# Scores of a windowed attention: two fp32r matmuls over split queries and keys, replaced by one float32 matmul on four array tiles

## The chip, the cores and the metric

One core of a Trainium2 chip. The metric is the time of one execution on the device in microseconds (us). TensorE (PE) multiplies, VectorE (DVE) and ScalarE (ACT) work elementwise, GpSimd (POOL) makes masks, and the SP queue starts most transfers.

## The reference

A decoder layer for 2048 positions and 1024 channels: half of the mixing channels go through a gated linear recurrence (4 heads), the other half through a sliding-window attention (8 query heads, 2 key/value heads of 64 channels); then an output projection, a gated feed-forward part with a short convolution, and a last normalisation. All in float32. The change touches the scores alone:

```python
scores = jnp.einsum('bnqhgd,bnkhd->bnhgqk', qb, kb) * scale   # blocks of 128 queries, 256 keys
dist = qi + ATT_BLOCK - kj
band = (dist >= 0) & (dist < WINDOW)                           # WINDOW = 128
scores = jnp.where(mask[None, :, None, None], scores, -jnp.inf)
m = jnp.maximum(jnp.max(scores, axis=-1, keepdims=True), sink)
p = jnp.exp(scores - m)
denom = jnp.sum(p, axis=-1, keepdims=True) + jnp.exp(sink - m)
```

Each block of 128 queries sees its own 128 keys and the 128 before. Of these 256 the band keeps exactly 128 for each query: keys at its own place or earlier in its own block, and later ones in the block before.

## The kernel before, in words

The sequence is worked in two halves of 1024 positions (`hf`). For each half there is a mixing stage (recurrence and attention, about 60 to 360 us and 1090 to 1410 us in the profile), an output projection (`out_proj`), and the feed-forward part (`gate_up`, `down`). The large products run as fp32r matmuls over operands that are split in a high and a low part (`unit`: hi·hi, hi·lo and lo·hi, 128 x 512 each, line 222; `project_v`, lines 750 to 752).

In the mixing stage a string of steps (`ORDER`) says in which order the generators are advanced: `H0` to `H3` are the recurrence's heads (`hgrn`), `A0` to `A3` the pairs of attention heads (`attend`), `V` the values' projection, `G` a gate's weights. A pair `j` holds one query head of each key/value head, the first in partitions 0 to 63, the second in 64 to 127 (`rows(kv)`). The order in which the instructions stand on each engine in the end is set by a scheduler that runs when the program is built, so a change in one place moves instructions around it.

The recurrence uses float32 matmuls on parts of the array: `pdiag` (128 rows, four tiles of 32 columns), `plev` (tiles of 32 or 64 columns). The attention's output product `poT` (line 541) uses two tiles of 64 columns. `pkn`, `pu`, `po`, `ppt`, `pot` are float32 with the whole array.

`attend` works on 512 queries at a time (`g`), for each kv head separately. It makes qh (fp32r) and ql (the rest) from q: qh stands in both halves of the partitions, and so does ql. `att_keys` makes the matching keys `KS`: for each kv, the high part in the head's own 64 rows and the low part in the other 64. A matmul of qh with `KS` then gives hi·hi and hi·lo at once, one of ql with `KS` the other two. For every two blocks of queries (`i0`) the scores go to one PSUM bank of the ring `at` (two banks, also used by `pv`, `ppt` and `poT`). From there ScalarE copies the scores of the earlier 128 keys to `sc`, and VectorE's predicated copy (mask `C.own`) puts those of the own block over them where the band says so: 128 numbers for each query are left. Then come the maximum, the exponentials and the sums, the transposes (`ppt`) and `poT`.

Of the kernel before, what the change touches and what calls it, by code (L numbers as in the profile page):

```python
# [17 lines left out]
P = 128  # L18
# [3 lines left out]
HALF = 1024  # L22
# [31 lines left out]
def hymba_layer(ctx: ExitStack, tc: tile.TileContext, a: dict, out: bass.AP):  # L54
# [19 lines left out]
    def ps(kind, name):  # L74
        return spaces[kind].tile([P, 512], F32, tag=kind, name=name)
# [33 lines left out]
    kc = cp.tile([P, 2, P], F32R, name="kcarry")  # L109
# [319 lines left out]
    def rows(kv):  # L429
        return slice(kv * HD, (kv + 1) * HD)  # L430

    def att_keys(hf, kv, invb, p):

        KS = p.tile([P, 2, P + HALF], F32R, name="KS")
        V = p.tile([P, 1 + TT, P], F32, name="V")
        if hf:
            nc.vector.tensor_copy(KS[:, :, 0:P], kc)  # L440
            nc.vector.tensor_copy(V[:, 0], vc)
        kT, vT = [p.tile([P, HALF], F32, tag="t4", name=n, bufs=2) for n in ("kT", "vT")]
        for jj, dst in ((ATT_J, kT), (ATT_J + 1, vT)):
            o = kv[jj - ATT_J]
            for b, bs in halves():
                nc.vector.tensor_tensor(dst[:, bs], o[b], invb[:, bs], op=ALU.mult)
                nc.scalar.activation(dst[:, bs], dst[:, bs], AF.Identity, bias=C.battn[:, jj:jj + 1])
        for kv in range(2):
            r, other = rows(kv), rows(1 - kv)
            nc.scalar.copy(KS[r, kv, P:], kT[r])  # L450
            nc.vector.tensor_tensor(KS[other, kv, P:], kT[r], KS[r, kv, P:].bitcast(F32), op=ALU.subtract)
        for b in range(NB):
            pv = ps("at", "pv")
            for i in range(4):
                t0 = (b * 4 + i) * P
                nc.tensor.transpose(pv[:, i * P:(i + 1) * P], vT[:, t0:t0 + P], ident)
            nc.scalar.copy(V[:, 1 + 4 * b:5 + 4 * b].rearrange("p a b -> p (a b)"), pv)
        if hf + 1 < NH:
            nc.vector.tensor_copy(kc, KS[:, :, HALF:HALF + P])
            nc.vector.tensor_copy(vc, V[:, TT])  # L460
        return KS, V

    def attend(hf, j, X, invb, KS, V, mix, p):

        o = unit(a["w_att"][j], X, "q")
        qT = slot(f"att{j}")
        for b, bs in halves():
            nc.vector.scalar_tensor_tensor(qT[:, bs], o[b], 0.125, invb[:, bs], op0=ALU.mult, op1=ALU.mult)
            nc.scalar.activation(qT[:, bs], qT[:, bs], AF.Identity, bias=C.bq[:, j:j + 1])
        yield  # L470
        scs = []
        for g in range(NB):
            sc = p.tile([P, 2, 4, P], F32, tag="sc", name="sc", bufs=2)
            gs = slice(g * 512, (g + 1) * 512)
            for kv in range(2):
# [3 lines left out]
                nc.scalar.copy(qh[r], qT[r, gs])  # L479
                nc.scalar.copy(qh[other], qT[r, gs])  # L480
                nc.vector.tensor_tensor(ql[r], qT[r, gs], qh[r].bitcast(F32), op=ALU.subtract)
                nc.scalar.copy(ql[other], ql[r].bitcast(F32))
                for i0 in (0, 2):
                    pb = ps("at", "psc")
                    first = hf == 0 and g == 0 and i0 == 0
                    for i in range(2):
                        n = g * 4 + i0 + i
                        w0 = 1 if first and i == 0 else 0
                        o = pb[:, i * 256 + w0 * P:(i + 1) * 256]
                        ks = slice((n + w0) * P, (n + 2) * P)  # L490
                        for t, qx in enumerate((qh, ql)):
                            nc.tensor.matmul(o, qx[:, (i0 + i) * P:(i0 + i + 1) * P], KS[:, kv, ks],
                                             start=t == 0, stop=t == 1)
                    pv = pb.rearrange("p (i w k) -> p i w k", i=2, w=2)
                    dst = sc[:, kv, i0:i0 + 2]
                    if first:
                        nc.vector.memset(dst[:, 0], NEG)
                        nc.scalar.copy(dst[:, 1], pv[:, 1, 0])
                    else:
                        nc.scalar.copy(dst, pv[:, :, 0])  # L500
                    nc.vector.copy_predicated(
                        dst, C.own.bitcast(U32).unsqueeze(1).to_broadcast([P, 2, P]), pv[:, :, 1])
# [13 lines left out]
            nc.scalar.activation(es, es, AF.Exp)  # L516
            nc.vector.tensor_tensor(den, den, es, op=ALU.add)
            nc.vector.reciprocal(den, den)
            nc.vector.tensor_tensor(sc, sc, den.unsqueeze(3).to_broadcast([P, 2, 4, P]), op=ALU.mult)
            scs.append(sc)  # L520
        yield
        for g, sc in enumerate(scs):
            pm = []
            for kv in range(2):
                pm.append([p.tile([P, 4, P], F32, tag="pp", name=n, bufs=4) for n in ("po", "pp")])
                pt = ps("at", "ppt")
                for i in range(4):
                    nc.tensor.transpose(pt[:, i * P:(i + 1) * P], sc[:, kv, i], ident)
                ptv = pt.rearrange("p (i q) -> p i q", i=4)
                for dst, mk in zip(pm[kv], (C.ownT, C.prevT)):  # L530
                    nc.vector.tensor_tensor(dst, ptv, mk.unsqueeze(1).to_broadcast([P, 4, P]), op=ALU.mult)
            oT = ps("at", "poT")
            first = None
            for i in (3, 2, 1, 0):
                n = g * 4 + i
                noprev = hf == 0 and n == 0
                for prev in (0,) if noprev else (1, 0):
                    for kv in (1, 0):
                        r = rows(kv)
                        with tc.issue_after(first) if first else ExitStack():  # L540
                            mm = nc.tensor.matmul(oT[r, i * P:(i + 1) * P], V[:, n + 1 - prev, r], pm[kv][prev][:, i],
                                                  start=noprev or prev == 1, stop=prev == 0)
# [706 lines left out]
    for hf in range(NH):  # L1249
        X, kv, invb, rs, f0 = nxt  # L1250
        with ExitStack() as st:
            p = pool(f"mix{hf}", stack=st, reuse_waits="tile")
            KS, V = att_keys(hf, kv, invb, p)
# [4 lines left out]
            pairs = [attend(hf, j, X, invb, KS, V, mix, p) for j in range(ATT_J)]  # L1258
# [85 lines left out]
```

## Time and profile before

| | us |
|---|---|
| median of 3 runs (lowest, highest) | 2125.06 (2124.44, 2128.92) |
| the profiled execution | 2124.22 |
| its span, first to last instruction | 2122.6 |
| TensorE busy in it | 2108.1 |
| VectorE, ScalarE busy | 1624.3, 1096.2 |

A matmul's busy time runs from its start to its modelled end, and matmuls overlap, so the sum over a group says less than the distance between starts; the timeline and the chain of waits give that. A plain float32 matmul of the program stands as two records in the trace (two passes over it), an fp32r one as one. In the timeline a row `x4` merges four neighbours, and its second number is the time from the first start to the last end.

### The profile page before, as it was taken

How to read it: one execution, taken by the hardware profiler on the slowest of the kernel's cores; microseconds unless marked ns; L12 is line 12 of the kernel's file. 1: busy time of each engine (PE TensorE's matmuls, PEld its weight loads, DVE VectorE, ACT ScalarE, POOL GpSimd, SP SyncE). 2: the span in 40 equal slices, each digit the busy share in tenths (PEclk: the TensorE clock that was granted, in tenths of full speed). 3: DMA queues.
4: the chain of work that ended last, by engine and by line, in shares of the span. 5: the costliest groups of instructions: out<-in, count | busy, mean ns of one | idle time of the engine just before them, and what ended most of it. 6: DMA issues, size and time to landing. Idle time of an engine off the chain costs nothing.

```text
span 2122.6 us, 29885 instructions
## 1 busy us (share of the span) xinstructions
PE 2108.1 (99%) x11584; PEld 1748.9 (82%) x11584; DVE 1624.3 (77%) x2374; ACT 1096.2 (52%) x1880; POOL 22.3 (1%) x52
## 2 busy tenths in 40 slices
PE   9999999999999999999999999999999999999998
PEld 7888888888888888888888888888888888878888
DVE  7457787898878878775863677868988787887766
ACT  6456575664434444335734476656544444443453
POOL 1000000000000000000000000000000000000000
PEclk9999999999999999999999999999999999999999
DMA  4111111523332325955731010213223223279643
GB/s 160 43 40 43 33 47 47 173 75 101 107 116 85 126 88 190 393 199 168 233 105 52 31 36 31 81 49 142 95 90 124 94 95 119 85 242 372 228 134 134
DMA packets 96475, 255.21 MB, mean 120 GB/s; under 512 B 17355, under 2 KB 19659, under 8 KB 96333
## 3 DMA queue, kind: packets, MB, share of 16 engines
q1 hardware_dynamic: 91076, 251.32, 34.4%
q10 hardware_dynamic: 5256, 1.98, 0.4%
q8 instruction: 91, 1.49, 0.3%
q14 instruction: 52, 0.42, 0.1%
HBM read 195.11 MB, written 57.16 MB: 119 GB/s over the span
## 4 chain that ended last, share of the span: by engine, by line
PE 97%; DVE 1%; ACT 1%; DMA 1%; issue 0%; SPq 0%; DVEq 0%; ACTq 0%
PE pop L222 8%; PE X L933 8%; PE X L934 8%; PE X L935 7%; PE q L222 4%; PE g L222 4%; PE f L222 4%; PE hq L222 4%; PE Y L935 4%; PE Y L933 4%; PE Y L934 4%; PE pdx L1151 3%; PE pdx L1153 3%; PE pdx L1152 3%; PE pdy L1151 3%; PE pdy L1152 3%
## 5 line engine op out<-in xcount | busy, mean ns | idle before, releaser
L758 ACT CAST whi<-raw 128x1024 fp32r<-128x1024 f32 x88 | 92.7, 1053 | 102.9 <-PE X L934 61.1
L933 PE MATMUL X<-T,whi 128*128 128x512 f32 x352 | 137.1, 389 | 0.0
L934 PE MATMUL X<-T,whi 128*128 128x512 f32 x352 | 136.9, 389 | 0.0
L935 PE MATMUL X<-T,wlo 128*128 128x512 f32 x352 | 136.9, 389 | 0.0
L1032 DVE SCALAR_TENSOR_TENSOR y<-ga,cw,y 128x1024 f32<-128x1024 f32 x88 | 112.6, 1281 | 28.4 <-ACT y L1030 28.2
L940 ACT COPY u<-X 128x512 f32<-128x512 f32 x88 | 51.7, 588 | 124.4 <-PE X L935 124.3
L200 ACT CAST whi<-raw 128x1024 fp32r<-128x1024 f32 x57 | 59.5, 1050 | 101.2 <-PE hq L222 33.5
L201 DVE TENSOR_TENSOR wlo<-raw,whi 128x1024 fp32r<-128x1024 f32 x57 | 69.4, 1222 | 54.8 <-ACT whi L200 54.5
L759 DVE TENSOR_TENSOR wlo<-raw,whi 128x1024 fp32r<-128x1024 f32 x88 | 107.4, 1221 | 0.3 <-ACT whi L758 0.3
L222 PE MATMUL pop<-XL,whi 128*128 128x512 f32 x256 | 88.7, 392 | 0.0
L631 ACT COPY G<-QK 128x1024 f32<-128x1024 f32 x48 | 51.4, 1070 | 71.7 <-DVE QK L653 66.5
L222 PE MATMUL pop<-XH,wlo 128*128 128x512 f32 x256 | 88.4, 391 | 0.0
L759 DVE TENSOR_TENSOR xld<-raw,xhd 128x1024 fp32r<-128x1024 f32 x72 | 81.1, 1134 | 9.3 <-ACT xhd L758 9.1
L222 PE MATMUL pop<-XH,whi 128*128 128x512 f32 x256 | 87.9, 394 | 0.0
L758 ACT CAST xhd<-raw 128x1024 fp32r<-128x1024 f32 x72 | 69.6, 978 | 27.1 <-DMA raw<-act0T 7.4
L933 PEld LDWEIGHTS X<-T,whi 128*128 128x128 f32 x352 | 66.1, 188 | 14.1 <-ACT u L940 0.4
L935 PEld LDWEIGHTS X<-T,wlo 128*128 128x128 f32 x352 | 66.1, 188 | 13.8
L934 PEld LDWEIGHTS X<-T,whi 128*128 128x128 f32 x352 | 66.0, 188 | 13.7
L1151 PE MATMUL pdx<-xhd,hid 128*128 128x512 f32 x192 | 74.5, 392 | 1.5 <-ACT xhd L758 0.9
L1152 PE MATMUL pdx<-xld,hid 128*128 128x512 f32 x192 | 74.7, 389 | 0.0
L653 DVE TENSOR_TENSOR QK<-QK,f 128x1024 f32<-128x1024 f32 x56 | 68.6, 1225 | 6.7 <-ACT G L631 5.9
L1153 PE MATMUL pdx<-xhd,lod 128*128 128x512 f32 x192 | 73.7, 389 | 0.0
(394 smaller groups left out, 6329.5 us busy)
## 6 DMA issues: line engine op xcount, KB each, us to landing
wr<-in_w_down SPq DMA_DIRECT2D x90, 512.0 KB, 4.9
raw<-in_w_gate SPq DMA_DIRECT2D x44, 512.0 KB, 3.5
raw<-in_w_up SPq DMA_DIRECT2D x44, 512.0 KB, 3.6
raw<-act0T SPq DMA_DIRECT2D x20, 512.0 KB, 5.0
raw<-act1T SPq DMA_DIRECT2D x20, 512.0 KB, 6.8
act0B<-y SPq DMA_DIRECT2D x33, 256.0 KB, 2.4
act1B<-y SPq DMA_DIRECT2D x33, 256.0 KB, 4.1
raw<-in_w_out SPq DMA_DIRECT2D x16, 512.0 KB, 4.4
```

The lines of the kernel that those rows point to most:

```text
L201: nc.vector.tensor_tensor(lo, raw, hi.bitcast(F32), op=ALU.subtract)
L222: marks["unit"] = nc.tensor.matmul(o[b], w, x[:, bs], start=f, stop=l)
L653: done = nc.vector.tensor_tensor(own, own, Fv.rearrange("p b w -> p w b").unsqueeze(3).to_broadcast([P, 2, nb, m]), op=ALU.mult)
L758: return (nc.scalar.copy(h, src), (eng or nc.vector).tensor_tensor(l, src, h.bitcast(F32), op=ALU.subtract))
L759: (eng or nc.vector).tensor_tensor(l, src, h.bitcast(F32), op=ALU.subtract))
L933: nc.tensor.matmul(o, wh[:, ws], xh, start=i == 0 and not more, stop=False, skip_group_check=more)
L934: nc.tensor.matmul(o, wh[:, ws], xl, start=False, stop=False, skip_group_check=more)
L935: r = nc.tensor.matmul(o, wl[:, ws], xh, start=False, stop=i == 3, skip_group_check=more)
L1032: nc.vector.scalar_tensor_tensor(y, g[:, w:w + HALF], C.cw[:, ft, w:w + 1], y, op0=ALU.mult, op1=ALU.add)
L1151: nc.tensor.matmul(o, wh[:, i, c], ah[:, i, cols], start=f, stop=False, skip_group_check=more)
L1152: nc.tensor.matmul(o, wh[:, i, c], al[:, i, cols], start=False, stop=False, skip_group_check=more)
L1153: nc.tensor.matmul(o, wl[:, i, c], ah[:, i, cols], start=False, stop=l, skip_group_check=more)
```

## The change

q and the keys are no longer split. `att_keys` leaves the keys in float32 (`Ks`), and `attend` computes the scores with plain float32 matmuls of 64 rows (one head's 64 channels) by 64 columns (half of a block's queries). There are four such tiles: kv 0 or 1 by rows, first or second half of the queries by columns. Each half of the queries meets the 192 keys that its band can reach, in place of 256. The two kv heads write to two PSUM banks, both of the ring `at`, in the same pass of the loop. The evacuation is cut by the halves of the queries, since each half's 192 keys begin at another place: the ScalarE copies bring the 128 earlier keys (two groups of 64, in reverse order for the second half), the predicated copies the 64 keys of the diagonal.

```diff
-        KS = p.tile([P, 2, P + HALF], F32R, name="KS")
+        Ks = p.tile([P, P + HALF], F32, name="Ks")
...
-        for kv in range(2):
-            r, other = rows(kv), rows(1 - kv)
-            nc.scalar.copy(KS[r, kv, P:], kT[r])
-            nc.vector.tensor_tensor(KS[other, kv, P:], kT[r], KS[r, kv, P:].bitcast(F32), op=ALU.subtract)
...
-            for kv in range(2):
-                r, other = rows(kv), rows(1 - kv)
-
-                qh, ql = [p.tile([P, 512], F32R, tag="pp", name=n, bufs=4) for n in ("qh", "ql")]
-                nc.scalar.copy(qh[r], qT[r, gs])
-                nc.scalar.copy(qh[other], qT[r, gs])
-                nc.vector.tensor_tensor(ql[r], qT[r, gs], qh[r].bitcast(F32), op=ALU.subtract)
-                nc.scalar.copy(ql[other], ql[r].bitcast(F32))
-                for i0 in (0, 2):
-                    pb = ps("at", "psc")
...
-                        for t, qx in enumerate((qh, ql)):
-                            nc.tensor.matmul(o, qx[:, (i0 + i) * P:(i0 + i + 1) * P], KS[:, kv, ks],
-                                             start=t == 0, stop=t == 1)
...
+            for i0 in (0, 2):
+                first = hf == 0 and g == 0 and i0 == 0
+                pbs = [ps("at", "psc") for _ in range(2)]
+                for i in range(2):
+                    n = g * 4 + i0 + i
+                    for qs in (0, HD):
+                        w0, w1 = P if first and i == 0 else qs, P + qs + HD
+                        for kv in range(2):
+                            marks["psc"] = nc.tensor.matmul(pbs[kv][qs:qs + HD, i * 256 + w0:i * 256 + w1],
+                                                            qT[rows(kv), n * P + qs:n * P + qs + HD],
+                                                            Ks[rows(kv), n * P + w0:n * P + w1], start=True, stop=True)
+                for kv in range(2):
+                    pv = pbs[kv].rearrange("p (i w k) -> p i w k", i=2, w=4)
+                    dst = sc[:, kv, i0:i0 + 2].rearrange("p i (w k) -> p i w k", w=2)
+                    c0 = 1 if first else 0
...
+                    nc.scalar.copy(dst[0:HD, c0:], pv[0:HD, c0:, 0:2])
+                    nc.scalar.copy(dst[HD:, c0:], pv[HD:, c0:, 2:0:-1])
+                    for w, r in enumerate((slice(0, HD), slice(HD, P))):
+                        mk = C.own[r, w * HD:(w + 1) * HD].bitcast(U32).unsqueeze(1).to_broadcast([HD, 2, HD])
+                        nc.vector.copy_predicated(dst[r, :, w], mk, pv[r, :, 2 + w])
```

How the instructions stand. On TensorE, the first score block of the program, before (`pvv` is the values' projection, `pkn` a transpose of the recurrence, tile numbers shown):

```order
L752 MATMUL pvv_989<-wlo_626,XH_282 128x512
L492 MATMUL psc_1028<-KS_449,qh_1022 128x128
L492 MATMUL psc_1028<-KS_449,ql_1023 128x128
L492 MATMUL psc_1028<-KS_449,qh_1022 128x256
L492 MATMUL psc_1028<-KS_449,ql_1023 128x256
L492 MATMUL psc_1036<-KS_449,qh_1022 128x256
L492 MATMUL psc_1036<-KS_449,ql_1023 128x256
```

The same place after (columns of the output's shape are partitions by keys):

```order
L743 MATMUL pvv_984<-wlo_621,XH_282 128x512
L479 MATMUL psc_1017<-Ks_449,att0_595 64x64
L479 MATMUL psc_1018<-Ks_449,att0_595 64x64
L479 MATMUL psc_1017<-Ks_449,att0_595 64x128
L479 MATMUL psc_1018<-Ks_449,att0_595 64x128
L479 MATMUL psc_1017<-Ks_449,att0_595 64x192
L479 MATMUL psc_1018<-Ks_449,att0_595 64x192
```

The matmuls now alternate between the two kv heads' banks (1017 and 1018) and between halves of the queries.

On TensorE, scores of head pair 1 in the first half, before (`g` is a gate's projection, `plev` the recurrence on 32 columns):

```order
L222 MATMUL g_1879<-XH,whi 128x512
L492 MATMUL psc<-KS,qh 128x128
L492 MATMUL psc<-KS,qh 128x256
L643 MATMUL plev<-G 32x32 x32
L492 MATMUL psc<-KS,ql 128x128
```

And after, from the second to the third score block of that pair:

```order
L479 MATMUL psc<-Ks,att_1702 64x192 x8
L222 MATMUL g_1861<-XH,whi 128x512
L222 MATMUL g_1862<-XH,whi 128x512
L222 MATMUL g_1861<-XL,whi 128x512
L222 MATMUL g_1862<-XL,whi 128x512
L222 MATMUL g_1861<-XH,wlo 128x512
L222 MATMUL g_1862<-XH,wlo 128x512
L222 MATMUL g_1861<-XH,whi 128x512
L222 MATMUL g_1862<-XH,whi 128x512
L628 MATMUL plev<-G 32x32 x16
L640 MATMUL plev<-G 64x64 x8
L479 MATMUL psc<-Ks,att_1702 64x192 x8
```

A block is now eight matmuls that take both banks, and here eight projection matmuls and two groups of `plev` stand between one block and the next.

On ScalarE after, around the evacuation of that second block (`G`, `moved`, `ST` belong to the recurrence):

```order
L622 COPY G<-QK 128x1024
L603 DMA odd<-moved 112x64
L489 COPY sc<-psc 64x256
L490 COPY sc<-psc 64x256
L489 COPY sc<-psc 64x256
L490 COPY sc<-psc 64x256
L652 COPY ST<-strip 32x8x32 x4
```

Four copies stand here in a row, where there were two of all 128 partitions; the casts of qh and ql are gone from this engine.

More of the change, by code (lines that the diff above doesn't have):

```diff
@@ L108, in hymba_layer @@
     nc.vector.memset(state, 0.0)
-    kc = cp.tile([P, 2, P], F32R, name="kcarry")
+    kc = cp.tile([P, P], F32, name="kcarry")
     vc = cp.tile([P, P], F32, name="vcarry")
@@ L432, in att_keys @@
     def att_keys(hf, kv, invb, p):
-        KS = p.tile([P, 2, P + HALF], F32R, name="KS")
+        Ks = p.tile([P, P + HALF], F32, name="Ks")
         V = p.tile([P, 1 + TT, P], F32, name="V")
         if hf:
-            nc.vector.tensor_copy(KS[:, :, 0:P], kc)
+            nc.vector.tensor_copy(Ks[:, 0:P], kc)
             nc.vector.tensor_copy(V[:, 0], vc)
-        kT, vT = [p.tile([P, HALF], F32, tag="t4", name=n, bufs=2) for n in ("kT", "vT")]
-        for jj, dst in ((ATT_J, kT), (ATT_J + 1, vT)):
+        vT = p.tile([P, HALF], F32, tag="t4", name="vT", bufs=2)
+        for jj, dst in ((ATT_J, Ks[:, P:]), (ATT_J + 1, vT)):
             o = kv[jj - ATT_J]
@@ L458, in att_keys, with attend @@
         if hf + 1 < NH:
-            nc.vector.tensor_copy(kc, KS[:, :, HALF:HALF + P])
+            nc.vector.tensor_copy(kc, Ks[:, HALF:HALF + P])
             nc.vector.tensor_copy(vc, V[:, TT])
-        return KS, V
-    def attend(hf, j, X, invb, KS, V, mix, p):
+        return Ks, V
+    def attend(hf, j, X, invb, Ks, V, mix, p):
         o = unit(a["w_att"][j], X, "q")
@@ L474, in attend @@
             gs = slice(g * 512, (g + 1) * 512)
-            for kv in range(2):
-                r, other = rows(kv), rows(1 - kv)
-                qh, ql = [p.tile([P, 512], F32R, tag="pp", name=n, bufs=4) for n in ("qh", "ql")]
[L479 to L482, printed above, removed]
-                for i0 in (0, 2):
-                    pb = ps("at", "psc")
[L485 to L490, printed above, removed]
-                        for t, qx in enumerate((qh, ql)):
-                            nc.tensor.matmul(o, qx[:, (i0 + i) * P:(i0 + i + 1) * P], KS[:, kv, ks],
-                                             start=t == 0, stop=t == 1)
-                    pv = pb.rearrange("p (i w k) -> p i w k", i=2, w=2)
-                    dst = sc[:, kv, i0:i0 + 2]
@@ L496, in attend @@
                     if first:
                         nc.vector.memset(dst[:, 0], NEG)
[L498 to L502, printed above, removed]
+                        nc.scalar.copy(dst[HD:, 0, 0], pv[HD:, 0, 2])
+                    nc.scalar.copy(dst[0:HD, c0:], pv[0:HD, c0:, 0:2])
@@ L1257, in hymba_layer @@
             heads = [hgrn(hf, h, X, invb, vs, WG, mix, p, f0 if h == 0 else None) for h in range(HG)]
-            pairs = [attend(hf, j, X, invb, KS, V, mix, p) for j in range(ATT_J)]
+            pairs = [attend(hf, j, X, invb, Ks, V, mix, p) for j in range(ATT_J)]
             wv = {}
```

2 lines of the change are left out of this document (1 added, 1 removed).

## The prediction

> **What bounds the kernel now.** I read the page first: the span, the busy times and the chain that ended last.
>
> ```profile
> span 2122.6 us, 29885 instructions
> PE 2108.1 (99%) x11584; PEld 1748.9 (82%) x11584; DVE 1624.3 (77%) x2374; ACT 1096.2 (52%) x1880; POOL 22.3 (1%) x52
> ...
> PE 97%; DVE 1%; ACT 1%; DMA 1%; issue 0%; SPq 0%; DVEq 0%; ACTq 0%
> ```
>
> TensorE carries 97% of the chain, so in the whole program time is the number of TensorE instructions times the spacing of their starts. The scores are computed in the two mixing stages. The table by stretches and the list of waits show whether another engine holds TensorE up there:
>
> ```profile
> 170.00:400.00 230.00, 228.66 (x1840) 190.73 (x1840) 176.10 (x342) 152.08 (x354) 4.03 (x6) 1.00 0.20 65
> 1180.00:1430.00 250.00, 249.09 (x1994) 208.64 (x1993) 188.09 (x365) 152.91 (x376) 4.67 (x9) 1.00 0.15 46
> ```
>
> ```profile
> engine line waited for: us in total, times, longest us
> PE poT L541 <- DVE y L180: 1.8, 2, 0.9
> ...
> PE po L715 <- DVE SS L701: 0.4, 1, 0.4
> ```
>
> In both stretches (length, then PE, weight loads, VectorE, ScalarE) TensorE is busy over 99% at granted clock 1.00, VectorE 75 to 77%, ScalarE 61 to 66%. The waits in these stages are 2.2 us together; the list's other rows are start-up and the down projection. Taking work off VectorE or ScalarE is therefore worth at most about 2 us. What decides is TensorE's own time for the scores, and I price it by starts, not by the durations in the groups, which overlap.
>
> **What is removed: 256 fp32r matmuls.** The group row gives the count, the chain the spacing:
>
> ```profile
> L492 PE MATMUL psc<-KS,qh 128*128 128x256 f32 x120 | 33.1, 301 | 0.0
> ```
>
> ```profile
> 114.34 0.94 PE psc L492 x8
> 115.28 0.87 PE pkn L688 x8
> ...
> 121.18 0.47 PE psc L492 x4
> ...
> 128.03 1.61 PE g L222 x7
> ```
>
> Four `psc` matmuls with 256 keys take 0.47 us, 0.1175 each. There are 240 of them (120 with qh, 120 with ql): 28.2 us. The other 16 (4 head pairs, 2 kv, 2 parts, in the first half's first block) have 128 keys: the first chain row is 0.94 for eight, of which two are these, so 0.94 less 6 x 0.1175 leaves about 0.11 for each, 1.8 us. Removed: 30.0 us.
>
> **What is added: 256 plain float32 matmuls of 64 rows by 64 columns.** 240 stream 192 keys, 8 stream 128, 8 stream 64. A plain float32 matmul is two records in the trace:
>
> ```profile
> L541 PE MATMUL poT<-po,V x256: 272/273/273, 148.0 to 1413.7; 128*64 128x128 f32 x128
> L541 PE MATMUL poT<-pp,V x240: 272/273/324, 147.8 to 1413.5; 128*64 128x128 f32 x120
> ```
>
> The program has 248 such calls of the output product, the trace 496 records. The price of a record depends on how many array tiles run at once. Three rows bound it. Serial, on the full array: `pkn` above, 0.109 us for a record of 128 columns. On two column tiles, `poT`:
>
> ```profile
> 148.02 0.39 PE L541 MATMUL poT<-po,V 128*64 128x128 f32 x4
> 148.24 0.39 PE L541 MATMUL poT<-pp,V 128*64 128x128 f32 x4
> 148.46 0.39 PE L541 MATMUL poT<-po,V 128*64 128x128 f32 x4
> ```
>
> Four records start every 0.22 us, so two tiles overlap fully. On four column tiles, `pdiag` (256 columns, then 128):
>
> ```profile
> 66.11 0.39 PE L222 MATMUL q<-XH,wlo 128*128 128x512 f32 x1
> 66.43 0.42 PE L586 MATMUL pdiag<-dd,ones 128*32 128x256 f32 x4
> ```
>
> ```profile
> 66.67 0.62 PE L586 MATMUL pdiag<-dd,ones 128*32 128x256 f32 x12
> 67.22 0.50 PE L750 MATMUL pvv<-whi,XH 128*128 128x512 f32 x1
> ```
>
> Four records of 256 columns share 0.24 us (the next four start at 66.67), and all sixteen, 768 columns for each tile, end with the next instruction at 67.22; less 0.15 us of leaving the mode (below) that is 0.64 us, 0.83 ns a column, the pace of one record. So four column tiles overlap fully too. For 192 columns a set of records takes 0.160 us, and a matmul of two records costs 0.080 us four wide, 0.165 two wide (0.11 times 192/128), 0.327 one after another. For the 240 matmuls that is 19.2, 39.6 or 78.5 us, and the 16 short ones add 0.6, 1.2 or 2.4.
>
> No row here shows two *row* tiles at once: every matmul before has 128 rows. I take four wide, 19.8 us: the nearest rows (`pdiag`, `poT`) overlap in full whatever the number of tiles, each tile has its own rows, columns and, for the two heads, its own PSUM bank, and in most blocks the order rotates through the four tiles. Two wide is kept as the upper end. Weight loads don't bind: `plev` with 64 columns (row 189.98 below) spends 0.62 us on sixteen load and matmul pairs, at most 0.039 each, against 0.040 a record needed.
>
> **What it adds in switching.** The scores were in the full-array form like the projections around them; now every run of them changes the array's form:
>
> ```profile
> 189.03 0.39 PE L222 MATMUL f<-XH,whi 128*128 128x512 f32 x1
> 189.35 0.70 PE L637 MATMUL plev<-G 128*32 128x32 f32 x32
> 189.98 0.69 PE L649 MATMUL plev<-G 128*64 128x64 f32 x16
> 190.60 0.33 PE L492 MATMUL psc<-KS,qh 128*128 128x128 f32 x1
> 190.76 0.28 PE L492 MATMUL psc<-KS,ql 128*128 128x128 f32 x1
> 190.87 0.33 PE L492 MATMUL psc<-KS,qh 128*128 128x256 f32 x1
> ```
>
> Entering: 189.03 to 189.35 is 0.32 where a projection's matmul takes 0.23 (1.61 for seven): 0.09. From one tile form to the next: 0.63 for sixteen pairs of 32 columns, which stream in 0.51 (0.83 ns times 2 records over 2 tiles, with a few ns of start): 0.12. Leaving: 0.62 for eight pairs of 64 columns, 0.47 of streaming, and then 0.16 for a 128-key `psc` instead of 0.06: 0.25. In the built order TensorE enters tile forms from the full array 52 times before and 67 after, leaves as often, and goes from one tile form to another 9 times before and 29 after (a score block often stands right behind a `plev` block). So 15 x (0.09 + 0.25) + 20 x 0.12 = 7.5 us, all on the path. Bounds: 0, if a change hides behind the last stream, to 50 x 0.25 = 12.5.
>
> **ScalarE and VectorE.**
>
> ```profile
> L479 ACT CAST qh<-att x32: 597/617/623, 71.1 to 1380.4; 64x512 fp32r<-64x512 f32 x32
> L480 ACT CAST qh<-att x32: 617/619/622, 71.8 to 1381.1; 64x512 fp32r<-64x512 f32 x32
> L481 DVE TENSOR_TENSOR ql<-att,qh x32: 671/686/690, 73.0 to 1381.3; 64x512 fp32r<-64x512 f32 x32
> L482 ACT CAST ql<-ql x32: 614/618/622, 74.9 to 1382.1; 64x512 fp32r<-64x512 f32 x32
> ...
> L501 DVE COPY_PREDICATED sc<-own,psc x64: 391/444/457, 115.3 to 1398.2; 128x256 f32<-128x256 uint32 x64
> L500 ACT COPY sc<-psc x56: 345/372/393, 116.5 to 1397.8; 128x256 f32<-128x256 f32 x56
> ...
> L450 ACT CAST KS<-kT x4: 1032/1038/1046, 43.0 to 1091.0; 64x1024 fp32r<-64x1024 f32 x4
> L451 DVE TENSOR_TENSOR KS<-kT,KS x4: 1219/1220/1221, 44.1 to 1092.3; 64x1024 fp32r<-64x1024 f32 x4
> ```
>
> ScalarE loses 32 x 1.854 + 4 x 1.04 = 63.5 us and gains 64 copies more than the 64 it had, at most 0.37 each: 23.8. VectorE loses 32 x 0.686 + 4 x 1.22 = 26.8 us and has 128 predicated copies of 128 elements a partition in place of 64 of 256: at most 64 x 0.444 = 28.4 more, at least nothing. Both lie beside TensorE; I cost the relief at nothing, since TensorE waits 2.2 us in all there, and the cover is TensorE's own projections. If VectorE kept all of the 28.4 us, its two mixing stretches would still be under 83% busy.
>
> **The new wait.** Both `at` banks are now taken by one block of eight matmuls (kv 0 and kv 1), so the next score block waits for the whole evacuation: four ScalarE copies (4 x 0.37) and, after the last, two predicated copies (at most 2 x 0.44): 2.4 us if nothing else is queued. The built order puts 2.5 us or more of other TensorE work in between; the tightest place, between the second and third block of head pair 1, has eight projection matmuls (8 x 0.23), a `plev` block of 0.63 us and 0.3 of switching, 2.8 us. What is queued behind a late block is everything on TensorE. About eight such close places, each between 0 and 0.9 us short (a 1.22 us VectorE operation standing in the way), bound it at 0 to 7 us; with the relief the lower end is -2. I take +1.5, nearer the lower end, since the list of waits before is so short.
>
> **Sum.** -30.0 + 19.8 + 7.5 + 1.5 = -1.2 us on a span of 2122.6, in an execution of 2124.22 us; that execution is 0.84 under the median of the three runs, 2125.06. From the median: 2123.9, and I say 2124. 0.2% is 4.25 us, about what this kernel's runs can tell (2124.44 to 2128.92).
>
> **Rivals.**
> *Two wide*: row halves of the array run after one another, or the two records of a matmul block the tile behind. Score time 40.8 instead of 19.8: +21, 2145. For it: no row shows row tiles together. Against: `pdiag`'s four tiles. It decides once a matmul costs over about 0.10 us.
> *About three wide*: the runs are short, eight matmuls, so that filling counts. At 0.107 us a matmul the scores take 26.5, so +6.7: 2130.5. For it: the first four `pdiag` records take 0.24 where the pace says 0.21. The Trainium skill, "TensorE: Matmul & The Clock Gate", section "Measured speedup vs the span model", gives 3.07 times for four row tiles, and a serial 0.327 over 3.07 is an estimate of 0.107. The trace so far speaks for fuller overlap, on column tiles alone.
> *Cheap switching*: the 64 by 64 form is entered and left behind streams still running. Without the 7.5 and the 1.5: 2115; with half of them, 2119.5. For it: 33 of the 37 score runs end before a full-array matmul whose load can go ahead. Against: row 190.60.
> *The bank pair*: the evacuation is late at most blocks, +7 instead of 1.5: 2129.5. For it: the 1.22 us VectorE operations. Against: the built order leaves 2.5 us or more, and q no longer waits for its split.
>
> **How the numbers follow.** Four wide as summed 0.56, own range 2120 to 2128; two wide 0.15; three wide 0.10; cheap switching 0.12; bank pair 0.07. Faster by over 0.2%: most of cheap switching and a tenth of the likeliest, 0.17. Slower: two wide, most of three wide and of the bank pair, and a little of the likeliest, 0.31. Within: 0.52. The range must reach two wide to hold 8 in 10: 2117 to 2145.
>
> **What will show it.** In the trace after, four `psc` records of 192 columns every 0.16 us confirm four wide, two say two wide; a block of eight should take 0.65 us to the last start. Around each block, starts stretched by 0.09 and 0.25 confirm the switching. Waits of TensorE's `psc` for the copies into `sc` beyond 2 us in all mean the bank pair. The groups of `qh`, `ql` and `KS` must be gone, with TensorE's idle time unchanged. The prediction is wrong if a score matmul costs over 0.10 us or a change of form over 0.4.

## The result, and the profile after

| | before | after |
|---|---|---|
| median of 6 runs each, us (lowest, highest) | 2124.95 (2123.9, 2128.92) | 2135.14 (2133.16, 2137.73) |
| profiled execution, its span, us | 2124.22, 2122.6 | 2133.16, 2131.4 |

The change costs 10.2 us: ratio 1.0046, 95% interval 1.0033 to 1.0059. I had forecast 2124 and no difference that can be told. The profiled execution of the changed kernel is the fastest of its six, so the two profiles that are compared below differ by 8.8 us.

The page of the changed kernel, span, busy times and chain:

```profile
span 2131.4 us, 30505 instructions
...
PE 2112.7 (99%) x11840; PEld 1736.2 (81%) x11840; DVE 1614.0 (76%) x2402; ACT 1062.9 (50%) x1852; POOL 22.1 (1%) x52
...
PE 93%; ACT 2%; DVE 2%; DMA 1%; issue 1%; ACTq 0%; SPq 0%; DVEq 0%
```

TensorE carries 93% of the chain instead of 97; ScalarE and VectorE stand in it with 2% each. The table by stretches (length, PE, weight loads, VectorE, ScalarE) shows that in the mixing stages:

```profile
170.00:400.00 230.00, 225.99 (x1914) 182.21 (x1914) 169.86 (x347) 136.21 (x341) 4.04 (x6) 1.00 0.19 62
1180.00:1430.00 250.00, 247.72 (x2097) 200.76 (x2097) 186.97 (x389) 144.61 (x380) 5.64 (x9) 1.00 0.13 41
```

TensorE idles 4.0 us in the first stretch (1.3 before) and 2.3 in the second (0.9 before), at granted clock 1.00, and ScalarE and VectorE have *less* work than before. So it is not the load of an engine but the moment at which something is done. The list of waits (total, times, longest) names the place:

```profile
PE psc L479 <- DVE sc L493: 3.2, 5, 1.1
...
PE psc L479 <- ACT moved L601: 0.7, 1, 0.7
```

The list counts only the part of a gap in which a semaphore was missing. For an account of everything I took the starts of all matmuls from both traces and subtracted from each distance the streaming pace of its form (41 ns for a 192-column record four wide, 118 ns for a 256-key fp32r matmul, and so on). A rest over 250 ns is called a gap; a smaller one at a change of the array's form, or right behind it, goes to the change.

| us, first to last matmul start | before | after | difference | predicted |
|---|---|---|---|---|
| score matmuls | 30.7 | 22.3 | -8.4 | -10.2 |
| changes of form, mixing stages | 16.5 | 26.1 | +9.6 | +7.5 |
| gaps over 250 ns, mixing stages | 3.5 | 10.6 | +7.1 | +1.5 |
| rest of the mixing stages | 689.8 | 689.8 | 0 | 0 |
| all other stages | 1374.7 | 1375.4 | +0.7 | 0 |
| sum | 2115.2 | 2124.2 | +9.0 | -1.2 |

**A block that is not disturbed**, in TensorE's timeline after:

```profile
120.01 0.61 PE L222 MATMUL g<-XH,whi 128*128 128x512 f32 x2
120.56 0.88 PE L479 MATMUL psc<-Ks,att 64*64 64x192 f32 x16
121.36 1.49 PE L688 MATMUL pu<-v,Kn 128*128 128x128 f32 x11
```

Eight matmuls stand as sixteen records. From their first start to the next instruction it is 0.80 us; the entry costs 0.09 (0.55 for two projections that take 0.46), and the first full-array record behind is about 0.11 late: 1.0 us, against 0.94 for eight fp32r matmuls in the prediction's first chain row. Even here, with streaming four wide, nothing is won.

**Two blocks that are disturbed**, TensorE, then ScalarE, then VectorE:

```profile
184.03 1.52 PE L479 MATMUL psc<-Ks,att 64*64 64x192 f32 x16 [0.67 <-DVE sc L493]
...
189.13 1.77 PE L479 MATMUL psc<-Ks,att 64*64 64x192 f32 x16 [0.29 <-DVE sc L493]
```

```profile
186.16 1.05 ACT L622 COPY G<-QK 128x1024 f32<-128x1024 f32 x1 [1.53 <-DVE QK L644]
...
187.11 0.36 ACT L489 COPY sc<-psc 64x256 f32<-64x256 f32 x1
187.48 0.37 ACT L490 COPY sc<-psc 64x256 f32<-64x256 f32 x1
187.87 0.37 ACT L489 COPY sc<-psc 64x256 f32<-64x256 f32 x1
188.25 0.37 ACT L490 COPY sc<-psc 64x256 f32<-64x256 f32 x1
```

```profile
187.23 1.23 DVE L644 TENSOR_TENSOR QK<-QK,f 128x1024 f32<-128x1024 f32 x1 [0.27 <-ACT G L622]
188.38 0.61 DVE L493 COPY_PREDICATED sc<-own,psc 64x128 f32<-64x128 uint32 x2
...
189.28 0.61 DVE L493 COPY_PREDICATED sc<-own,psc 64x128 f32<-64x128 uint32 x2
```

The block of 184.03 has its last record at 185.24. ScalarE then stands idle for 1.53 us, since the copy to `G` is ahead of the score copies in its queue and waits for VectorE. The copies run from 187.11; the predicated copies of kv 0 stand behind a 1.23 us product until 188.38. The first bank is free at 189.0, the second at 189.9: 4.6 us after the block where I had counted 2.4. The next block begins at 189.13 on the first bank and stops in the middle for the second.

At 341.54 the two banks come free still further apart, TensorE and ScalarE:

```profile
341.54 0.54 PE L479 MATMUL psc<-Ks,att 64*64 64x192 f32 x2
343.18 0.87 PE L479 MATMUL psc<-Ks,att 64*64 64x192 f32 x14 [1.10 <-DVE sc L493]
```

```profile
338.08 0.37 ACT L490 COPY sc<-psc 64x256 f32<-64x256 f32 x1
338.48 1.65 ACT L652 COPY ST<-strip 32x256 f32<-32x256 f32 x4
340.13 1.28 ACT L507 ACT_TABLE_LOAD   x1
...
341.64 0.37 ACT L489 COPY sc<-psc 64x256 f32<-64x256 f32 x1
```

Between the copies of kv 0 and of kv 1 stand four copies to `ST` and a table load. TensorE alternates between the two banks, so it stops after two records. Six blocks of 32 are like this (184.0, 189.1, 341.5, 1240.5, 1245.6, 1390.5); their late entries and stops, 0.8 to 1.4 us at each, make up the 7.0 us of gaps at `psc` (0.3 before).

### The profile page after: what moved, and what is told of

Read it like the earlier page. It is cut to its first block, busy times and chain, and to the rows that moved or that the text cites. A ratio compares the mean times of both kernels' runs of the same rounds, so it can differ in the third digit from the quotient of the medians.

```text
span 2131.4 us, 30505 instructions
## 1 busy us (share of the span) xinstructions
PE 2112.7 (99%) x11840; PEld 1736.2 (81%) x11840; DVE 1614.0 (76%) x2402; ACT 1062.9 (50%) x1852; POOL 22.1 (1%) x52
## 3 DMA queue, kind: packets, MB, share of 16 engines
q8 instruction: 93, 1.52, 0.3%
## 4 chain that ended last, share of the span: by engine, by line
PE 93%; ACT 2%; DVE 2%; DMA 1%; issue 1%; ACTq 0%; SPq 0%; DVEq 0%
PE pop L222 8%; PE X L924 7%; PE X L925 7%; PE X L926 7%; PE hq L222 4%; PE q L222 4%; PE f L222 4%; PE Y L925 4%; PE Y L924 4%; PE Y L926 4%; PE g L222 4%; PE pdx L1142 3%; PE pdx L1144 3%; PE pdx L1143 3%; PE pdy L1142 3%; PE pdy L1144 3%
```

## The experiments

The theory after the result was the bank pair: streaming and changes of form as priced, and the surplus in the waits for the two banks. The rivals were a higher price of the matmuls (two or three wide) and of the changes. Each was first measured by itself. Times are medians; ratios are to the kernel before on the same chip, which took 2124.1 to 2124.9 us each time.

### The matmul's price: every score matmul twice

```diff
-                            marks["psc"] = nc.tensor.matmul(pbs[kv][...
+                            for _ in range(2):
+                                marks["psc"] = nc.tensor.matmul(pbs[kv][...
```

> Every score matmul of the changed kernel is issued twice into the same place, so the scores are unchanged and only their streaming doubles. If the four array tiles work at once (0.080 us a matmul), 240 more matmuls of 192 keys and 16 short ones add 19.8 us: about 2155 against the changed kernel's 2135. If the tiles worked in twos, 40.8 us: 2176. If the extra time over the kernel before is per block (changes of form, waits for the banks) it stays as it is and the slope is the streaming alone.

2168.3 us, 1.0212 (1.0198 to 1.0226): 33 us over the changed kernel. That lies between the two forecasts, so the time alone does not decide. An undisturbed block in the timeline does:

```profile
120.92 1.59 PE L480 MATMUL psc<-Ks,att 64*64 64x192 f32 x32
122.44 2.05 PE L689 MATMUL pu<-v,Kn 128*128 128x128 f32 x16
```

1.52 us for 32 records against 0.80 for 16: eight more matmuls cost 0.72, 0.090 each. That is four wide (two wide was 0.165). 256 of them make 23 us. Of the other 10, about 8 lie in score blocks that the built order cut in pieces (45 score runs instead of 37): sixteen records of one kv head, for which only two tiles run, take 1.5 us to the next instruction, as long as a whole block of 32. About 2 are new gaps; the changes of form cost no more than before the doubling (169 of them for 163).

### The price of a change of form: a tiny tile matmul ahead of each block, in the kernel before

```diff
                     pb = ps("at", "psc")
+                    nc.tensor.matmul(pb[0:HD, 0:HD], ident[0:HD, 0:HD], ident[0:HD, 0:HD], start=True, stop=True)
```

> The kernel before with one float32 matmul of 64 rows by 64 columns by 64 columns put ahead of each of its 64 score blocks, into a bank that the block overwrites: the change of form alone, with banks, splits and evacuation as before. The built order has 39 more entries and 39 more exits and 20 more steps between tile forms. Theory B (0.09 in, 0.25 out, 0.12 between): 15.7 us, and 64 x 0.107 = 6.8 us for the small matmuls themselves: 2147. If a change of form is nearly free: 2130 to 2132. If it costs double: 2163.

2148.35, 1.0113 (1.0099 to 1.0127): +23.5. The timeline of one:

```profile
121.39 0.40 PE L222 MATMUL g<-XH,wlo 128*128 128x512 f32 x1
121.71 0.33 PE L485 MATMUL psc<-ident 64*64 64x64 f32 x2
121.97 0.39 PE L493 MATMUL psc<-KS,qh 128*128 128x256 f32 x1
122.19 0.28 PE L493 MATMUL psc<-KS,ql 128*128 128x256 f32 x1
122.31 0.27 PE L493 MATMUL psc<-KS,qh 128*128 128x256 f32 x1
```

In: 0.32 where a projection takes 0.23. Out: 0.26 from the tiny matmul's start, and the first full-array matmul takes 0.22 instead of 0.12. That is 0.45 us for the pair, and it holds the tiny matmul's own streaming; less the 0.107 expected for that, it is the 0.34 of the prediction. The account puts 21.1 us to 98 more changes (113 to 211), again with most of that streaming in it; counted again with 0.107 us for each of the 64 tiny matmuls it leaves about 16 us, 0.16 each. The time agrees: 22.5 us were expected, and 1.9 of the 23.5 are new gaps. In the changed kernel 50 more changes cost 9.6 us, 0.19 each, a quarter above what I had taken.

### The pair of banks: before's matmuls with both banks at once, and the second bank from another ring

```diff
             for i0 in (0, 2):                      # kernel before, kv inside the block
+                pbs = [ps("at", "psc") for _ in range(2)]
```

> The kernel before with both kv heads' banks taken together and their fp32r matmuls ahead of both evacuations, as the changed kernel does: the bank pair alone, no change of form. Theory A: some 4 to 6 us of waits at the blocks: 2129 to 2131, with TensorE waiting for the copies into sc. Theory B: 2125, as before.

2127.09, 1.0013 (1.0004 to 1.0021): +2.2, gaps 6.8 us instead of 3.5, 2.1 of them at `psc`. With one copy and one predicated copy for each bank the pair costs a little, less than the 4 to 6 us expected if it alone made the waits.

```diff
-                pbs = [ps("at", "psc") for _ in range(2)]
+                pbs = [ps(k, "psc") for k in ("at", "mm")]     # changed kernel, kv 1 in the projections' ring
```

> The changed kernel with the second kv head's bank taken from the projections' ring of four banks, so that a score block takes one bank of the ring of two and the next block can begin while this one is evacuated. Theory A (TensorE waits at the blocks for the evacuation of both banks): the waits of the score matmuls for the copies into sc, 3.2 us by the list and about 6 by the gaps, go: 2129 to 2130. Theory B (the changes of the array's form are the cost): only what the order changes, 12 entries and exits fewer and 8 steps between tile forms more, about -3: 2132. Theory C (neither; the order elsewhere): 2135.

2176.21, 1.0246 (1.0232 to 1.026). The waits of TensorE:

```profile
PE psc L479 <- DVE sc L493: 8.2, 4, 3.1
PE pkn L679 <- ACT ST L666: 4.4, 2, 3.1
PE psc L479 <- ACT att L465: 4.4, 4, 1.7
```

The projections' ring then holds the scores up as well, and the other way round: 50 us of gaps. This run says nothing on the cause.

### A cheaper or earlier release of the banks

Four edits of the changed kernel. ScalarE copies each bank raw, GpSimd and VectorE put the keys in place from there:

```diff
+                    raw = p.tile([P, 512], F32, tag="pp", name="scr", bufs=4)
...
+                            nc.scalar.copy(raw[r].rearrange("p (i k) -> p i k", i=2)[:, :, o:o + 192],
+                                           pbs[kv][r].rearrange("p (i k) -> p i k", i=2)[:, :, o:o + 192])
...
-                    nc.scalar.copy(dst[0:HD, c0:], pv[0:HD, c0:, 0:2])
+                    nc.gpsimd.tensor_copy(dst[0:HD, c0:], pv[0:HD, c0:, 0:2])
```

> The changed kernel, but ScalarE takes each bank's scores to SBUF as they are (two copies of 384 numbers a partition for a bank), and GpSimd and VectorE arrange them there: a bank is free after two ScalarE copies, without VectorE. Theory A (TensorE's 8.2 us of gaps at the score blocks are waits for the two banks): the part that waits for VectorE's predicated copies goes, some 4 us, against 0.8 us more of changing form: 2132. If it is ScalarE's queue that holds the second bank, the same wait is now for ScalarE: 2135. Theory B (form changes alone): 2136.

Only kv 0 evacuated, zeros in the place of kv 1's scores:

```diff
-                for kv in range(2):
+                nc.gpsimd.memset(sc[:, 1, i0:i0 + 2], 0.0)
+                for kv in range(1):
```

> The changed kernel with the second kv head's scores computed but not evacuated; GpSimd fills their place with zeros, so half of the output product is of no meaning. The second bank is free at once, and ScalarE and VectorE have half of the evacuation. Theory A: most of the 8.2 us of gaps at the blocks goes, less 2.3 us for 5 more entries and exits and 5 more steps between tile forms: 2129. Theory B: 2137.

All 256 keys for each half of the queries, with the evacuation of the kernel before (one copy, one predicated copy for each bank):

```diff
-                            nc.tensor.matmul(pbs[kv][qs:qs + HD, i * 256 + w0:i * 256 + w1], ...
+                            nc.tensor.matmul(pbs[kv][qs:qs + HD, i * 256 + w0:(i + 1) * 256], ...
...
```

> The changed kernel with all 256 keys for each half of the queries and the evacuation of the kernel before: one ScalarE copy and one predicated copy of 128 partitions a bank in place of two and two. Streaming at four wide rises by 240 x 0.027 = 6.4 us, form changes by about 1. If the cutting of the evacuation makes the waits (8.2 us, of which some 6 would go): 2136 to 2137. If the waits come from what stands between the two banks' copies on ScalarE and VectorE: 2142.

Kv 1's copies on VectorE:

```diff
+                    cp_ = nc.vector.tensor_copy if kv else nc.scalar.copy
-                    nc.scalar.copy(dst[0:HD, c0:], pv[0:HD, c0:, 0:2])
+                    cp_(dst[0:HD, c0:], pv[0:HD, c0:, 0:2])
...
```

> The changed kernel with the second kv head's copies out of the bank on VectorE (which then does its predicated copies) and the first's on ScalarE. VectorE gets 19 us more, ScalarE 24 us less. If the second bank is held since ScalarE's four copies of a block do not stand together (a table load and other copies in between), the gaps at the blocks shrink by some 5 us: 2131. If VectorE is what holds it: 2136 or more.

| | us | ratio | gaps, us (at `psc`) |
|---|---|---|---|
| raw copies | 2143.19 | 1.0086 (1.0072, 1.01) | 14.1 (1.3) |
| kv 0 alone | 2148.89 | 1.0111 (1.0095, 1.0126) | 15.1 (2.0) |
| 256 keys | 2152.1 | 1.0131 (1.0117, 1.0145) | 28.6 (10.5) |
| two engines | 2136.97 | 1.0056 (1.0043, 1.0068) | 9.5 (2.8) |

One line of TensorE's waits from each, in the same order:

```profile
PE ppt L529 <- POOL sc L499: 5.3, 2, 2.8
```

```profile
PE pu L689 <- ACT Kn L681: 5.6, 3, 2.6
```

```profile
PE psc L479 <- DVE sc L490: 6.7, 4, 3.4
```

```profile
PE ppt L520 <- DVE sc L494: 2.5, 3, 1.3
```

Three of the four brought the wait at `psc` down, and none brought the time down; only the last came out where one of its forecasts had it (2136 or more, if VectorE is what holds the bank). The wait stood at the next consumer instead (`ppt`, `pu`), and where a bank came free alone the built order cut blocks into halves of one kv head: eight records, which take 0.80 us to the next instruction like a whole block of sixteen, since only two tiles run (18 such halves with kv 0 alone, 14 with two engines, 4 in the changed kernel). Half of the evacuation left out makes the kernel 14 us *slower*. So the length of the evacuation is not the cause by itself.

### Evacuation first, blocks held together

```diff
+                with tc.high_priority():
                     for kv in range(2):
                         pv = pbs[kv].rearrange("p (i w k) -> p i w k", i=2, w=4)
```

> The changed kernel with the whole evacuation of a score block (ScalarE's copies and VectorE's predicated copies) taken ahead of other work that is ready on those engines when the program is built; the matmuls are unchanged, and TensorE's order nearly so (35 score runs for 37, 157 changes of form for 163, which is worth 6 x 0.17, about 1 us). Theory A, the banks come free late because other ScalarE and VectorE work stands ahead of a block's evacuation: TensorE's gaps at psc (7 us over 250 ns in the changed kernel) fall to under 3 and the time goes down by 4 to 6 us, to 2129-2131. Rival B, what was put back on ScalarE and VectorE (exponentials, copies, the recurrence's G and strip) is then late for TensorE by as much: psc's gaps fall, others at pu, plev or ppt come up, and the time is 2133-2137. Rival C, the evacuation itself is too long (four copies of 0.37 and two or three predicated copies of 0.30): psc's gaps stay and the time is 2134-2136.

```diff
-                        for kv in range(2):
-                            marks["psc"] = nc.tensor.matmul(pbs[kv][...
+                        for kv in (1, 0):
+                            with tc.issue_after(gate) if gate else ExitStack():
+                                mm = nc.tensor.matmul(pbs[kv][...
+                            gate = gate or mm.ins
```

> The changed kernel with the eight matmuls of a block held together behind the first, which goes to the second bank: a block begins only when both banks are free, and TensorE does other work until then where its order has some. 38 score runs, 164 changes of form. If stopping in the middle of a block (one bank free, the other not) is what the wait costs beyond the lateness itself, the time is 2129-2132. If only the lateness counts, the same wait stands at the block's entry instead and the time is 2134-2137.

Both:

> Both edits together: evacuation ahead of other work, blocks held together. 37 score runs, 161 changes. With theory A and no new waits 2127-2130, the level that the undisturbed blocks and the changes of form alone give: 2125 less 30.0, plus 19.8 of matmuls, plus about 11 of form changes (50 more of them) is 2126, plus 1 to 4 us of waits. With rival B 2133-2137.

2135.49 (1.0048, 1.0035 to 1.0061), 2135.63 (1.0049, 1.0035 to 1.0062) and 2136.91 (1.006, 1.0047 to 1.0072): no gain. Evacuation first leaves 6.9 us of gaps at `psc`:

```profile
PE psc L479 <- DVE sc L494: 3.7, 5, 1.2
PE ppt L520 <- DVE sc L511: 1.6, 2, 1.2
```

These are about the figures of rival C, the too long evacuation, but at the late block of 189 us it is still the order that holds the copies. VectorE in this run:

```profile
187.19 0.23 DVE L611 COPY_PREDICATED strip<-lmask,odd 120x64 f32<-120x64 uint32 x1 [1.20 <-DMA odd<-moved]
187.34 1.22 DVE L645 TENSOR_TENSOR QK<-QK,f 128x1024 f32<-128x1024 f32 x1
188.47 0.60 DVE L494 COPY_PREDICATED sc<-own,psc 64x128 f32<-64x128 uint32 x2
```

ScalarE has finished kv 0's copies at 187.03, but VectorE waits for a transfer of the recurrence first and then works its product, both ahead of the predicated copies in the built order. So "first among the ready" when the program is built did not put the copies first where it counted. Held together, the blocks wait 3.5 us at `psc`, and `plev`, `ppt` and `pkn` come up: 9.1 in all. Stopping in the middle by itself is not what costs.

### The recurrence's long steps cut in two

```diff
-                nc.scalar.copy(G.rearrange("p t (b c m) -> p t b c m", c=2, m=m), far)
+                for t in range(2):
+                    nc.scalar.copy(G.rearrange("p t (b c m) -> p t b c m", c=2, m=m)[:, t], far[:, t])
...
-            done = nc.vector.tensor_tensor(own, own, Fv.rearrange("p b w -> p w b")...
+            for t in range(2):
+                done = nc.vector.tensor_tensor(own[:, t], own[:, t], Fv[:, :, t]...
```

In the changed kernel, then with the evacuation first, then in the kernel before:

> The changed kernel with the recurrence's two long steps cut in two instructions each: ScalarE's copy to G (1.05 us, L622) and VectorE's product on QK (1.23 us, L644), first the query part, then the key part; same work and results. 39 score runs, 165 changes of form for 163. Theory A (the queues): at 184, 189, 1240 and 1245 us the evacuation of a score block stood behind one of these two steps in ScalarE's or VectorE's queue; with half of the step in front, each wait is up to 0.5 us shorter, psc's gaps fall from 7 to 3-5 us and the time is 2131-2134. Rival B (no slack is there to be had; the recurrence's level chain, now with more instructions, holds TensorE up itself): psc's gaps stay or plev's come up by 1-3 us, 2135-2138.

> The same cut together with the evacuation ahead of other ready work. 34 score runs, 158 changes of form. Theory A: the evacuation now waits for half a step at most and nothing else is ahead of it, psc's gaps 2-4 us, 2129-2132. Rival B: 2134-2138, with the gaps moved to plev, pu, ppt or pkn.

> The kernel before with the same cut, as the control: 110 changes of form for 113. It had 3.5 us of gaps in the mixing stages, 0.3 of it at psc. Theory A: nothing waits for these steps, so 2123.5-2126, the same. Rival B: the longer level chain shows here too, 2126-2129.

2142.67 (1.0088, 1.0074 to 1.0102), 2139.32 (1.007, 1.0058 to 1.0083) and, the control, 2129.61 (1.0025, 1.0015 to 1.0034). Theory A of these expectations falls: the gaps at `psc` are 5.6 and 6.4, and all gaps 12.2 and 13.9. All three times lie above rival B's range too. The control's waits:

```profile
PE po L717 <- DVE SS L703: 3.9, 2, 2.0
PE poT L541 <- DVE pp L531: 1.5, 4, 0.5
```

The kernel before, whose score matmuls are untouched, gets 8.1 us of gaps instead of 3.5. So such waits can come without any change of the scores; whether from the longer chain of the recurrence or from the disturbed order, this run does not tell.

### Two other orders for both kernels

The string of steps with the scores of most pairs one recurrence step later, in both kernels (the first line of `ORDER`'s difference, `H0 A0` for `A0 H0`, stands for four such places), and with the scores one step earlier:

```diff
-H0 A0 W0 H0 V0 G0 A0 H0 H0 A0 H0 H1 A0 H1 A1 G1 A1 H1 H1 A1 ...
+H0 A0 W0 H0 V0 G0 H0 A0 H0 A0 H0 H1 A0 H1 A1 G1 H1 A1 H1 A1 ...   (later)
+H0 A0 W0 A0 H0 V0 G0 H0 H0 A0 H0 H1 A0 A1 A1 H1 G1 H1 H1 A1 ...   (earlier)
```

> The changed kernel with another string of steps: in each half the scores of head pairs 0, 1 and 2 come one recurrence step later, behind the level rounds instead of among them, and pair 3's one step later too. 41 score runs, 172 changes of form for 163 (9 more, about +1.5 us). Theory A (the waits at psc come from where these scores stand, among the level rounds with their 1.05 us and 1.23 us steps): psc's gaps fall from 7 us to under 3 and the time is 2130-2134. Rival B (no slack in any order): 2136-2142, the gaps at psc as long as before or moved.

> The kernel before with the same later string, as the control: 114 changes of form for 113, the matmuls the same. If its order had been worth nothing special, 2124-2126. If any other order costs this kernel waits, as cutting the long steps did (+5), 2127-2132, and then part of what the change cost is the loss of an order that fitted.

> The changed kernel with the scores one recurrence step earlier, ahead of the level rounds. 35 score runs, 164 changes of form (44 of them from tile form to tile form, 29 in the changed kernel; 120 in and out for 134), worth about -0.6 us. Theory A: the evacuation comes ahead of the level rounds' steps in the queues, psc's gaps under 3 us, 2129-2133. Rival B: 2134-2142.

> The kernel before with the same earlier string, as its control. Here it splits the recurrence's tile blocks by score matmuls: 167 changes of form for 113, of them 56 more in or out, 28 pairs of 0.34 us: +9.5 us, and 2 fewer between forms. 2133-2136 from the form changes alone; above that it is waits.

| order | before, us | after, us | gaps before, after | changes of form before, after |
|---|---|---|---|---|
| as it was | 2124.95 | 2135.14 | 3.5, 10.6 | 113, 163 |
| later | 2124.81 (1.0004, 0.9995 to 1.0013) | 2134.54 (1.0049, 1.0035 to 1.0063) | 5.1, 9.3 | 114, 172 |
| earlier | 2133.16 (1.0041, 1.0028 to 1.0053) | 2138.73 (1.0063, 1.005 to 1.0075) | 3.1, 13.4 | 167, 164 |

Each kernel's largest entry for the mixing stages in the list of waits, with the later order (before, then after), and after with the earlier one:

```profile
PE poT L541 <- DVE y L180: 1.8, 2, 0.9
```

```profile
PE psc L479 <- DVE sc L493: 2.3, 4, 0.7
```

```profile
PE pu L688 <- ACT Kn L680: 6.2, 2, 3.1
```

The later order is the cleanest pair: the matmuls as in the originals, the kernel before as fast as it was, and the change again costs 9.7 us. So the loss does not hang on the one order. Its parts shift, though: here the gaps rise by 4.2 us only (4.2 of the 9.3 at `psc`, so theory A's "under 3" is missed), and there are 58 more changes of form instead of 50. The earlier order does what theory A asked for, gaps at `psc` of 1.5 us, and pays at `pu` (6.5) and `plev` (4.8) instead. And the kernel before, with as many changes of form as the changed one, loses 9 us with 3.1 us of gaps: the changes' price again, 0.17 each for 54 more, without the waits.

## Why the prediction was wrong

**The step that failed is "The new wait".** It took +1.5 of a bound of 0 to 7 and the gaps grew by 7.1, to 10.6 us, of which 7.0 are at `psc`. I had about eight close places, each 0 to 0.9 us short; the runs show six late blocks of 32, 0.8 to 1.4 us each. The rival "the bank pair" (+7, 2129.5) had the right place and size, with a chance of 0.07, though it expected most blocks to be late; the sign named for it, waits of `psc` for the copies beyond 2 us, is there with 3.2 us. Two things in the working of this step did not hold. The evacuation's length was added up as if its instructions stood together; in the queues they stand behind `G`, `QK`, `ST` and a table load, 4.6 us instead of 2.4 at 185 us. And I leaned on the short list of waits before, which said how well the *old* order fitted, not what a new order would leave. In the fourteen versions with tile scores measured here the gaps are 9.1 us or more, in the kernel before and its controls 3.1 to 8.1.

What stays open is how the 7 us divide. The pair of banks with the old matmuls cost 2.2 us. Cutting two steps cost the old kernel 5 without touching its scores, another order of the same steps nothing that can be told. So a disturbed order can cost as much as the banks, and need not; no version here separates the two in the changed kernel.

**Changes of form**: +7.5 predicted, +9.6 measured, inside the bounds of 0 and 12.5. The counts (50 more) were exact; the price is 0.19 for a change instead of the 0.15 that my mix of 0.09, 0.25 and 0.12 comes to. With the old matmuls the price was about right: 0.16 in the tiny-matmul run, 0.17 in the kernel before with the earlier order. Where the rest comes from in the changed kernel, no run here shows. "Cheap switching" is out by the tiny-matmul run.

**The matmuls**: -10.2 predicted, -8.4 measured. Four wide is right, two wide is out: 0.090 us by doubling, 0.087 in the account (22.3 for 256, the 16 short ones among them), where the sum had 0.080 and "three wide" 0.107. Against the serial 0.327, 0.090 is 3.6 times. The Trainium skill, "TensorE: Matmul & The Clock Gate", section "Measured speedup vs the span model", has 3.07 for four row tiles; in this mixed form, two by rows and two by columns, the trace shows more.

**Relief of ScalarE and VectorE**: costed at nothing, and that was right: in the two stretches they lost 24 and 7 us of work, and nothing else in the mixing stages became faster (689.8 and 689.8).

**The sum**: +5.6 from the wait, +2.1 from the changes, +1.8 from the matmuls and +0.7 elsewhere lead from -1.2 to +9.0. All four went the same way. The gain of the matmuls (8.4) is smaller than what the changes of form take (9.6), so with no more gaps than before the kernel would still stand at about 2127 (2125 less 8.4, plus 9.6 and 0.7). None of the versions beats the kernel before. That 2135 still lies inside 2117 to 2145 is luck: the range reached so far for two wide, which did not come; the likeliest case had 2120 to 2128.

## What to carry to other kernels

Price a new array form by the block, entry and exit included: here an 0.8 us block with 0.2 us at its ends equals the 0.94 us of the old form, however well the tiles overlap inside. When a change makes one matmul group need two buffers at once, follow the release through the in-order queues of the engines that give it (what stands ahead, and what that waits for), and do not just add up durations. Short waits in the old order say little of the order that a builder will make after the edit: run the same disturbance on the old kernel as a control.

## What the hardware showed beyond what I expected

Row tiles and column tiles overlap in full: in the undisturbed block of 120.56 the records start in fours, within 20 ns, and from the second four on each four takes 0.163 us (the first takes 0.21). Cutting an evacuation by partitions buys nothing here on either engine, as the groups' rows show:

```profile
L493 DVE COPY_PREDICATED sc<-own,psc x128: 283/302/311, 115.9 to 1404.0; 64x128 f32<-64x128 uint32 x128
L489 ACT COPY sc<-psc x64: 259/366/376, 115.3 to 1402.9; 64x256 f32<-64x256 f32 x56, 64x128 f32<-64x128 f32 x8
```

A ScalarE copy of 256 numbers on 64 partitions takes 366 ns, as on 128 before (372), and a predicated copy of half the elements a partition 302 instead of 444, so two of them take 604.
